# A hybrid attention block: six of the projection's nine column chunks in seven-product blocks, and attention moved behind them

## The chip, the cores and the metric

One Trainium2 chip, one of its cores. The time is that of one execution on the device, in microseconds. Both kernels compute in float32: every matrix product is written as three products of a high and a low part (hi·hi, hi·lo, lo·hi).

## The reference

One layer over 512 tokens of width 2048 with two kinds of attention heads (A: 8 query heads on 2 key/value heads; B: 8 heads of their own):

```python
h = rmsnorm(x, g_mix)
qa, ka, va, qb, kb, vb = split(h @ w_in)        # 1024,256,256,1024,1024,1024 columns
out_a = rmsnorm(mixer_a(qa, ka, va, ...))       # q, k normed per head, axial rotary, softmax
out_b = rmsnorm(mixer_b(qb, kb, vb))            # partial rotary; three dilated windows, as one masked softmax
x = x + concat(out_a, out_b) @ w_out
h2 = rmsnorm(x, g_ffn); gate, up = split(h2 @ w_gate_up)
x = x + (silu(gate) * up) @ w_down
return rmsnorm(x, g_final)
```

## The kernel before

Tokens lie in NT = 4 tiles of 128 rows, x is held transposed in KD = 16 tiles. The program is a hand-ordered list of *units*. A unit multiplies one weight tile of 128 x 512. Units of the first two phases, the input projection (w_in, 9 chunks of 512 columns x 16 units) and the output projection (w_out, 4 chunks for A, then 4 for B, x 8 units), have 12 matmuls: 4 token tiles times 3 products (`mm3`). The feed-forward (w_gate_up, w_down) runs in column blocks (`ColBlock`): of two column halves and two row halves, seven products of sums and differences take the place of eight plain ones, so a unit has 6 matmuls and there are 7 x 8 units for each pair of 512-column chunks and 16 row tiles. Its weights are first added or subtracted on DVE (L771).

Every weight tile is split: ACT copies it to a rounded high part (`split_hi`, L235 or L734), DVE subtracts that to get the low part (`split_lo`, L240 or L737). `prepare` issues the splits some units ahead and the loads (SP's queue) further ahead.

Attention is cut into small *tasks* in one queue, `side`. After every unit the main loop runs **one** task. `push_head` writes the tasks of a head: `m0` (transpose q on PE and split it, `tq`; finish the head before last: `pv(3)`, `fin`), `tk` (the same for k), and four score tasks `ms(i)`. A score task holds, in this order, `score(i)` of the current head, `pt(i)` of the head before and `pv(i-1)` of the head before:

- `score(i)`: 3 matmuls on PE (tile sc), row maximum on DVE (nm), exponential with row sum on ACT, reciprocal on DVE (L447), and p scaled by it on DVE (L448)
- `pt(i)`: 4 transposes on PE (tile pt), high part pTh on ACT (L186), low part pTl on DVE (L187)
- `pv(i-1)`: 3 matmuls on PE (tile o) that read pTh and pTl of the task before.

q and k of A are normed and turned on DVE (`push_norm_rope`, L312 to L328, two tasks for each of four token tiles), q and k of B turned by `rope_partial` (L383 to L387). Every engine takes its instructions in the order in which they are written. All q, k, v stay in SBUF, or go straight from PSUM into split form (`post_kvA`, `post_vB`); tasks of a head are queued as soon as its chunk of the projection is done.

Of the kernel before, what the change touches and what calls it, by code (L numbers as in the profile page):

```python
# [19 lines left out]
P = 128  # L20
# [30 lines left out]
RAWS = {"raw": 6, "craw": 24, "craw40": 23, "draw6": 22, "draw8": 28}  # L51
# [4 lines left out]
EVICT = 6  # L56

# [6 lines left out]
def encoder_block(ctx, tc, x, g_mix, w_in, g_q_a, g_k_a, g_out_a, g_out_b, w_out, g_ffn,  # L64
# [6 lines left out]
    sm = ctx.enter_context(tc.tile_pool(name="small", bufs=1))  # L71
# [14 lines left out]
    def wslot(tag):  # L86
        if tag == "wa":
            ring[0] += 1
            return home(16 + ring[0] % 12)
        return sp.tile([P, 512], F32R, tag=tag, bufs=W_TILES[tag], name=nm("w"))  # L90
# [4 lines left out]
    def small(base, n=4):  # L95
        return sm.tile([P, 16], F32, tag="t", bufs=24, name=nm(base))[:, :n]
# [7 lines left out]
    ident = cp.tile([P, P], F32, name="ident")  # L104
    gm = cp.tile([P, KD], F32, name="gm")
    gf = cp.tile([P, KD], F32, name="gf")
    go = cp.tile([P, KD], F32, name="go")
    mask = cp.tile([P, S + S - P], F32, name="mask")
    ropeb = cp.tile([P, 2, NT, PARTIAL], F32, name="ropeb")
    ones = cp.tile([P, 1], F32, name="ones")  # L110
    mhalf = cp.tile([P, 16], F32, name="mhalf")
    gqk = cp.tile([P, 2, HD], F32, name="gqk")
# [5 lines left out]
    def home(n):  # L118
        return form_tile(n % 7, n // 7).rearrange("p a b -> p (a b)")
# [5 lines left out]
    warm = slot("warm", BF16, (P, 512))  # L125
# [26 lines left out]
    def load_consts():  # L152
        for i, g in enumerate((g_q_a, g_k_a)):
            nc.sync.dma_start(gqk[:, i, :], row_bcast(g, HD))
        yield
# [3 lines left out]
        yield  # L159
        nc.sync.dma_start(ropeb, c_partial)  # L160
        yield
        nc.sync.dma_start(mask, c_mask)
        yield
# [9 lines left out]
    def rsqrt_mean(ss, n, count, name):  # L173
        t = small(name + "m", n)
        nc.vector.tensor_scalar(t, ss, 1.0 / count, EPS, op0=OP.mult, op1=OP.add)
        r = small(name, n)
# [3 lines left out]
    def split(src, name, gain=None, between=None, at=None):  # L180
        if at is None:
            hi, lo = slot(name + "h", F32R), slot(name + "l", F32R)
        else:
            hi, lo = home(at), home(at + 1)
# [3 lines left out]
        else:  # L188
            nc.scalar.activation(hi, src, AF.Copy, scale=gain)
            if between is not None:  # L190
                between()
# [62 lines left out]
    xT = [None] * KD  # L254
    ssx = slot("ssx")

    def x_transposes(k):
        ps = bank("xt")
        for t in range(NT):
            nc.tensor.transpose(ps[:, t * P:(t + 1) * P], xs[k][:, t, :], ident)  # L260
        if k == 0:
            xT[k] = split(ps, "xT", gm[:, k:k + 1], at=0)
            nc.scalar.activation(ssx, ps, AF.Square)
        else:
            sq = slot("xsq")
            xT[k] = split(ps, "xT", gm[:, k:k + 1], lambda: nc.scalar.activation(sq, ps, AF.Square), 2 * k)
            nc.gpsimd.tensor_tensor(ssx, ssx, sq, op=OP.add)
# [9 lines left out]
    def make_r1():  # L277
        r1["r"] = rsqrt_mean(col_sums(ssx), NT, D, "r1")
        r1["rs"] = small("r1s")
# [4 lines left out]
    def push_tables():  # L284
        for i, name in enumerate(("k", "q")):
# [15 lines left out]
            side.extend(lambda a=a, f=part: f(a) for a in range(3))  # L301

    def push_norm_rope(q0, dst, t, nh, name):
# [3 lines left out]
        def first():  # L307
            gs = tabs[name][1]
            tmp = st["tmp"] = slot("ra")
            ss = small("ssq")  # L310
# [4 lines left out]
            st["rs"] = rsqrt_mean(ss[:, :nh], nh, HD, "rq")  # L315
# [7 lines left out]
        def second():  # L323
            gc = tabs[name][0]
# [5 lines left out]
        side.extend((first, second))  # L330

    qA, kA, kTA, vA = {}, [], {}, {}
    vB, qkB = {}, {}
    kTA_done = []

    def post_kvA(ps):
        for j in range(2):
            vA[j] = tuple(home(48 + 2 * j + i).rearrange("p (a b) -> p a b", a=2) for i in range(2))
        for t in range(NT):
            r = r1["r"][:, t:t + 1]  # L340
            k0 = slot("kA")
            src = ps[t][:, 256:]
            h, l = vA[t // 2]
            nc.scalar.activation(h[:, t % 2, :], src, AF.Copy, scale=r)
            nc.scalar.activation(k0[:, :256], ps[t][:, :256], AF.Copy, scale=r)
            nc.vector.scalar_tensor_tensor(l[:, t % 2, :], src, r, f32(h[:, t % 2, :]), op0=OP.mult, op1=OP.subtract)
            kA.append(k0)
        for t in range(NT):
            push_norm_rope(kA[t][:, :256], kA[t][:, 256:], t, NKV, "k")
        wait(1)  # L350
        for kv in range(NKV):
            side.append(lambda kv=kv: transpose_k_a(kv))

    def transpose_k_a(kv):
# [3 lines left out]
        kTA[kv] = split(ps, "kT", at=52 + 2 * kv)  # L358

    def post_qA(j, ps):  # L360
        for t in range(NT):
            q0 = slot("qA")
            nc.scalar.activation(q0, ps[t], AF.Copy, scale=r1["r"][:, t:t + 1])
            push_norm_rope(q0, q0, t, 4, "q")
            qA[j, t] = q0
        wait(2)
        for h in range(4):
            push_head(("A", 4 * j + h))

    def post_vB(j, ps):  # L370
        for t in range(NT):
            r = r1["r"][:, t:t + 1]
            h, l = home(32 + 2 * (NT * j + t)), home(33 + 2 * (NT * j + t))
            nc.scalar.activation(h, ps[t], AF.Copy, scale=r)
            nc.vector.scalar_tensor_tensor(l, ps[t], r, f32(h), op0=OP.mult, op1=OP.subtract)
            vB[j, t] = (h, l)

    def rope_partial(q0, t):
        rot = q0.rearrange("p (h d) -> p h d", h=4)[:, :, :PARTIAL]
        tmp = sm.tile([P, 4, PARTIAL], F32, tag="rope", bufs=2, name=nm("rope"))  # L380
# [7 lines left out]

    def post_qkB(j, ps):
        for t in range(NT):  # L390
            q0 = qkB[j, t] = slot("qkB")
            nc.scalar.activation(q0[:, :256], ps[t][:, :256], AF.Copy, scale=r1["rs"][:, t:t + 1])
            nc.scalar.activation(q0[:, 256:], ps[t][:, 256:], AF.Copy, scale=r1["r"][:, t:t + 1])
        for t in (0, 2):
            side.append(lambda t=t: (rope_partial(qkB[j, t], t), rope_partial(qkB[j, t + 1], t + 1)))
        wait(1)
        for h in range(2):
            push_head(("B", 2 * j + h))
# [7 lines left out]
    class Head:  # L406
# [5 lines left out]
        def tq(self):  # L412
            ps = bank("qt")
            for t in range(NT):
                if self.kind == "A":
                    src = qA[self.h // 4, t][:, (self.h % 4) * HD:(self.h % 4 + 1) * HD]
                else:
                    src = qkB[self.h // 2, t][:, (self.h % 2) * HD:(self.h % 2 + 1) * HD]
# [3 lines left out]
        def tk(self):  # L422
# [4 lines left out]
            for t in range(NT):  # L427
                lo = 256 + (self.h % 2) * HD
                nc.tensor.transpose(ps[:, t * P:(t + 1) * P], qkB[self.h // 2, t][:, lo:lo + HD], ident)
            self.k = split(ps, "kT")  # L430

        def score(self, t):
            if t == 0:
                self.negm, self.z, self.rz = small("nm"), small("z"), small("rz")
# [13 lines left out]
            nc.vector.tensor_scalar(p, p, rz, None, op0=OP.mult)  # L448
# [10 lines left out]
        def pv(self, kb):  # L459
# [5 lines left out]
            else:  # L465
                v = cols(vB[self.h // 4, kb], (self.h % 4) * HD)
            mm3(self.o, v, self.pTs.pop(kb), kb == 0, kb == NT - 1)

        def fin(self):
# [12 lines left out]
            if self.h == 7:  # L482
                wait(1)
                side.append(lambda: row_rms(self.kind))
# [3 lines left out]
    def row_rms(kind):  # L488
        ro[kind] = rsqrt_mean(col_sums(acc[kind]), NT, NHA * HD, "ro")

    def push_head(spec):
        n = len(heads)
        heads.append(Head(*spec))

        def at(i, f, *a):
            return (i, f, a)
# [4 lines left out]
        def m0():  # L501
            cur.tq()
            if prev2:
# [9 lines left out]
        side.append(m0)  # L513
        side.append(cur.tk)
        for i in range(NT):
            side.append(lambda i=i: ms(i))
        if n == 15:
# [8 lines left out]
            side.append(t0)  # L526
            for i in range(NT):
                side.append(lambda i=i: tail(i))
# [4 lines left out]
            side.append(t5)  # L533
# [15 lines left out]
    def in_chunk(pieces, post):  # L549
        box = {}  # L550

        def mm(u, k):
            if k == 0:
                box["ps"] = [bank("pj") for _ in range(NT)]
            for t in range(NT):
                mm3(box["ps"][t], cols(xT[k], t * P), u.w, k == 0, k == KD - 1)
        add_chunk(w_in, [k * P for k in range(KD)], pieces, mm, lambda: post(box["ps"]), tag="wi")

    QB, KB, VB = 1536, 2560, 3584
    in_chunk([(1024, 0, 512)], post_kvA)  # L560
    in_chunk([(0, 0, 512)], lambda ps: post_qA(0, ps))
    in_chunk([(512, 0, 512)], lambda ps: post_qA(1, ps))

    def qk_pieces(j):
        return [(QB + 256 * j, 0, 256), (KB + 256 * j, 256, 256)]
    in_chunk([(VB, 0, 512)], lambda ps: post_vB(0, ps))
    in_chunk(qk_pieces(0), lambda ps: post_qkB(0, ps))
    in_chunk(qk_pieces(1), lambda ps: post_qkB(1, ps))
    in_chunk([(VB + 512, 0, 512)], lambda ps: post_vB(1, ps))
    in_chunk(qk_pieces(2), lambda ps: post_qkB(2, ps))  # L570
    in_chunk(qk_pieces(3), lambda ps: post_qkB(3, ps))

    x1 = {}
    oS = {}
    ss2 = small("ss2", 16)

    def drain_until(cond):
        while not cond():
            side.popleft()()

# [3 lines left out]
    def out_chunk(kind, c):  # L584
# [4 lines left out]
        def early(k):  # L589
            if (kind, k) not in oS:  # L590
                drain_until(lambda: (kind, k) in oT)
                oS[kind, k] = split(oT.pop((kind, k)), "oS", go[:, base + k:base + k + 1],
                                    at=42 + 2 * k if k < 7 else 35)

        class Back:
# [8 lines left out]
            def split(self):  # L604
                oS[kind, self.k] = split(self.t, "oS", go[:, base + self.k:base + self.k + 1],
                                         at=2 * self.k + (0 if kind == "A" else 42))
# [47 lines left out]
    def pair_sums(w):  # L654
# [3 lines left out]

        def tt(out, x, y, op=OP.subtract):
# [469 lines left out]
```

## Time and profile before

| what | value |
|---|---|
| time, median of 3 runs | 2025.89 us (2025.15 to 2027.72) |
| the profiled execution | 2026.94 us, its span 2025.2 us |
| mean granted TensorE clock | 0.997 |
| PE busy | 2005.7 us (99%), 9123 instructions |
| DVE busy | 1474.1 us (73%) |
| ACT busy | 1051.6 us (52%) |
| POOL busy | 134.9 us (7%) |

The input projection with most of the attention behind it ends near 590 us, the output projection near 720 us, and the feed-forward takes the rest. PE is the matrix engine, DVE and ACT are the two elementwise engines. A duration of a row in the timeline overlaps that of the next row on the same engine: what an instruction costs its engine is the distance from its start to the next start.

### The profile page before, as it was taken

The page shows a single profiled execution, that of the slowest core. Times are in us where ns is not written, and L with a number is a line of the kernel's source. Part 1 is how long each engine was busy: PE and PEld are TensorE (multiplying, and loading weights), DVE is VectorE, ACT ScalarE, POOL GpSimd, SP SyncE. Part 2 cuts the span into 40 slices and gives each one's busy share as a digit, 9 for nine tenths or more (in the row PEclk, how much of TensorE's full clock was granted, in tenths as well). Part 3 has the DMA queues.
Part 4 walks back from the last instruction along what each step waited for, and adds up shares of the span by engine and source line. Part 5 has one row for each costly group of instructions (what it writes and reads, how often), then busy time and mean ns, then how long its engine had stood idle before and what let it go on. Part 6 is the DMA issues. An engine that isn't in the chain of part 4 may idle for free. (4 is left out here: it accounts for less than half of the span.)

```text
span 2025.2 us, 26727 instructions
## 1 busy us (share of the span) xinstructions
PE 2005.7 (99%) x9123; PEld 1652.5 (82%) x9123; DVE 1474.1 (73%) x2596; ACT 1051.6 (52%) x1872; POOL 134.9 (7%) x149
## 2 busy tenths in 40 slices
PE   9999999999999999999999999999999999999997
PEld 7888888888888888888888888888888887788885
DVE  5555755554754688878877878878779987887876
ACT  5324344443543565555555555555556665666655
POOL 3100100000000000000000000000000121111121
PEclk9999999999999999999999999999999999999998
DMA  7322322223433546657558567467477799768754
GB/s 236 106 80 70 98 74 73 79 78 96 147 113 130 205 142 217 206 167 267 193 195 267 166 222 255 152 221 253 153 253 254 207 248 265 205 158 256 212 124 165
DMA packets 210360, 354.90 MB, mean 175 GB/s; under 512 B 19072, under 2 KB 63920, under 8 KB 210224
## 3 DMA queue, kind: packets, MB, share of 16 engines
q1 hardware_dynamic: 189440, 304.10, 45.9%
q0 software_dynamic: 12544, 25.17, 7.0%
q10 hardware_dynamic: 8240, 23.93, 3.5%
q8 instruction: 71, 1.16, 0.2%
q14 instruction: 65, 0.53, 0.1%
HBM read 300.97 MB, written 52.17 MB: 174 GB/s over the span
## 5 line engine op out<-in xcount | busy, mean ns | idle before, releaser
L734 ACT ACTIVATE tw<-raw 128x512 fp32r<-128x512 f32 x924 | 559.3, 628 | 442.5 <-DVE raw L771 280.7
L737 DVE TENSOR_TENSOR tw<-raw,tw 128x512 fp32r<-128x512 f32 x924 | 619.1, 686 | 173.4 <-ACT tw L734 169.5
L197 PE MATMUL zc<-tw,arena 128*128 128x512 f32 x1056 | 416.1, 394 | 2.0 <-ACT ev L907 1.9
L198 PE MATMUL zc<-tw,arena 128*128 128x512 f32 x1056 | 413.6, 392 | 3.5 <-DVE tw L737 3.5
L199 PE MATMUL zc<-tw,arena 128*128 128x512 f32 x1056 | 413.1, 391 | 0.0
L771 DVE TENSOR_TENSOR raw<-raw,raw 128x512 f32<-128x512 f32 x528 | 361.3, 684 | 0.5 <-DMA raw<-in_w_gate_up_dram 0.5
L198 PEld LDWEIGHTS zc<-tw,arena 128*128 128x128 f32 x1056 | 199.3, 189 | 46.7 <-DVE tw L737 6.5
L197 PEld LDWEIGHTS zc<-tw,arena 128*128 128x128 f32 x1056 | 199.1, 189 | 43.9 <-ACT ev L907 3.0
L199 PEld LDWEIGHTS zc<-tw,arena 128*128 128x128 f32 x1056 | 199.1, 189 | 41.5
L197 PE MATMUL pj<-w,arena 128*128 128x512 f32 x576 | 229.0, 398 | 1.2 <-ACT w L235 1.2
L198 PE MATMUL pj<-w,arena 128*128 128x512 f32 x576 | 224.8, 390 | 0.9 <-DVE w L240 0.9
L199 PE MATMUL pj<-w,arena 128*128 128x512 f32 x576 | 225.5, 391 | 0.1
L198 PE MATMUL yc<-tw,arena 128*128 128x512 f32 x528 | 206.0, 390 | 0.8 <-DVE tw L737 0.8
L197 PE MATMUL yc<-tw,arena 128*128 128x512 f32 x528 | 206.8, 392 | 0.0
L199 PE MATMUL yc<-tw,arena 128*128 128x512 f32 x528 | 205.8, 390 | 0.0
L240 DVE TENSOR_TENSOR w<-raw,w 128x512 fp32r<-128x512 f32 x176 | 130.8, 753 | 21.4 <-ACT w L235 13.6
L908 POOL DMA_DIRECT2D x1d<-ev x76 | 67.4, 990 | 1155.3 <-ACT ev L907 1149.4
L235 ACT ACTIVATE w<-raw 128x512 fp32r<-128x512 f32 x176 | 106.5, 627 | 56.1 <-PE pj L199 32.0
L199 PEld LDWEIGHTS pj<-w,arena 128*128 128x128 f32 x576 | 108.2, 188 | 23.9 <-DVE arena L192 0.5
L197 PEld LDWEIGHTS pj<-w,arena 128*128 128x128 f32 x576 | 108.3, 188 | 23.6 <-ACT w L235 1.4
L198 PEld LDWEIGHTS pj<-w,arena 128*128 128x128 f32 x576 | 108.5, 188 | 23.2 <-DVE w L240 1.2
L198 PEld LDWEIGHTS yc<-tw,arena 128*128 128x128 f32 x528 | 99.2, 188 | 21.8 <-DVE tw L737 1.6
(189 smaller groups left out, 2539.0 us busy)
## 6 DMA issues: line engine op xcount, KB each, us to landing
raw<-in_w_gate_up_dram SPq DMA_DIRECT2D x616, 256.0 KB, 4.5
raw<-in_w_down_dram SPq DMA_DIRECT2D x176, 256.0 KB, 6.7
forms<-pair SPq DMA_DIRECT2D x22, 896.0 KB, 5.2
raw<-in_w_in_dram SPq DMA_DIRECT2D x38, 512.0 KB, 3.7
x1d<-ev POOLq DMA_DIRECT2D x76, 256.0 KB, 6.6
fr<-forms ACTq DMA_DIRECT2D x35, 512.0 KB, 4.5
raw<-in_w_in_dram SPq DMA_DIRECT2D x68, 256.0 KB, 3.0
raw<-in_w_out_dram SPq DMA_DIRECT2D x32, 512.0 KB, 4.9
```

The costliest lines, as they stand in the source:

```text
L197: nc.tensor.matmul(dst, ah, bh, start=start, stop=False, skip_group_check=chained)
L198: nc.tensor.matmul(dst, ah, bl, start=False, stop=False, skip_group_check=chained)
L199: nc.tensor.matmul(dst, al, bh, start=False, stop=stop, skip_group_check=chained)
L235: nc.scalar.activation(self.w[0], src, AF.Copy)
L240: nc.vector.tensor_tensor(self.w[1], self.src, f32(self.w[0]), op=OP.subtract)
L734: nc.scalar.activation(self.pair[:, 0], self.src, AF.Copy)
L737: nc.vector.tensor_tensor(self.pair[:, 1], self.src, f32(self.pair[:, 0]), op=OP.subtract)
L771: nc.vector.tensor_tensor(t[dst], t[src[0]], t[src[1]], op=OP.add if form == "m6" else OP.subtract)
L908: nc.gpsimd.dma_start(x1_dram[2 * cb + j, row], e, accum_op=OP.add)
```

## The change

- Three pairs of chunks of the input projection (qA0+qA1, vB0+vB1, qB0+kB0) run as `ColBlock`s with seven products (`in_block`); kvA stays plain in front of them, qB1 and kB1 stay plain behind them. For this, x also gets sums and differences of its tile pairs (`x_prep`, `x_sums`, `x_split`) during the first chunk; one of x's plain parts that these overwrite goes to DRAM and comes back before qB1.
- All results of the projection are scaled, stored to DRAM from POOL's queue (`store`) and loaded back for attention on SP's queue (`reload`, `load_vB`).
- Attention begins only after the three blocks: `attention_tasks` queues all 161 tasks there, and over the next 64 units (qB1, kB1, and the four A chunks of the output projection) the loop runs `HEAD_RATE` = 2.7 tasks a unit.
- In `score`, p is scaled by the reciprocal on ACT and no longer on DVE.
- The row sums of squares for the first norm come from x loaded again by rows (4 x 1 MB) and squared on ACT with a row sum; before, POOL added squares of the transposed x, and PE summed them.
- v of B is split on ACT and DVE from the reloaded copy, one more task a head.
- Small tiles share one SBUF tile; two rings of weight buffers are a little shorter (`craw40` 23 to 20, `draw6` 22 to 20).

```diff
+HEAD_RATE = (2.7, 2.7)
+COLUMN_BLOCKS = 3
...
-            nc.vector.tensor_scalar(p, p, rz, None, op0=OP.mult)
+            nc.scalar.activation(p, p, AF.Copy, scale=rz)
...
+    in_plain("kvA", 1024)
+    groups = [(("qA0", "qA1"), (0, 512)), (("vB0", "vB1"), (VB, VB + 512)), (("qB0", "kB0"), (QB, KB)),
+              (("qB1", "kB1"), (QB + 512, KB + 512))]
+    for names, lo in groups[:COLUMN_BLOCKS]:
+        in_block(names, lo)
+    last = blocks[-1]
+    last.after("m7", 1, lambda: nc.gpsimd.dma_start(arena[0][:, 1], ar_dram))
+    last.after("m5", 0, load_consts)
+    last.after("m3", 0, lambda: side.extend(attention_tasks()))
...
+    attend = [len(units)]
+    for names, lo in groups[COLUMN_BLOCKS:]:
+        for name, c in zip(names, lo):
+            in_plain(name, c)
...
-        if side:
+        credit = credit + HEAD_RATE[n >= attend[1]] if attend[0] <= n < attend[2] else 1.0
+        while side and credit >= 1.0:
             side.popleft()()
+            credit -= 1.0
```

The new task list of a head, and the order in which the lists follow:

```diff
+        tasks = [m0] + ([cur.tk] if cur.kind == "B" else [])
+        tasks.extend(lambda i=i: ms(i) for i in range(NT))
...
+        todo = [lambda: reload("kvA", kA), lambda: reload("qA0", qA[0])] + table_tasks()
+        for t in range(NT):
+            todo += [lambda t=t: split_vA(t)]
+            todo += norm_rope(lambda t=t: (kA[t][:, :256], kA[t][:, 256:]), t, NKV, "k")
+        k_turns = [lambda kv=kv: transpose_k_a(kv) for kv in range(NKV)]
+        todo += q_tasks(0) + k_turns
+        for h in range(4):
+            todo += head_tasks(("A", h))
+            if h == 1:
+                todo += [lambda: reload("qA1", qA[1])]
+            if h == 2:
+                todo += q_tasks(1)
...
+        for h in range(8):
+            if h < 7:
+                todo.append(lambda h=h: load_vB(h + 1))
+            todo.append(lambda h=h: split_vB(h))
+            todo += head_tasks(("B", h))
```

DVE, two score tasks of an A head in the program before; sc is the score tile, nm its negative row maximum, rz the reciprocal of the row sum, pTl the low part of the transposed p, w a weight's low part:

```order
L440 TENSOR_REDUCE nm_2345<-sc_2435 128x1
L447 RECIPROCAL rz_2347<-z_2346 128x1
L448 TENSOR_SCALAR p_2439<-p_2439,rz_2347 128x512
L187 TENSOR_TENSOR pTl_2450<-pt_2444,pTh_2449 128x512
L240 TENSOR_TENSOR w_2408<-raw_2238,w_2407 128x512
L440 TENSOR_REDUCE nm_2345<-sc_2476 128x1
L447 RECIPROCAL rz_2347<-z_2346 128x1
L448 TENSOR_SCALAR p_2480<-p_2480,rz_2347 128x512
```

DVE, three score tasks of an A head in the changed program (nm, z and rz are now parts of smalls):

```order
L490 TENSOR_REDUCE smalls<-sc_3896 128x1
L497 RECIPROCAL smalls<-smalls 128x1
L193 TENSOR_TENSOR pTl_3911<-pt_3905,pTh_3910 128x512
L490 TENSOR_REDUCE smalls<-sc_3918 128x1
L497 RECIPROCAL smalls<-smalls 128x1
L193 TENSOR_TENSOR pTl_3933<-pt_3927,pTh_3932 128x512
L490 TENSOR_REDUCE smalls<-sc_3939 128x1
L497 RECIPROCAL smalls<-smalls 128x1
L193 TENSOR_TENSOR pTl_3954<-pt_3948,pTh_3953 128x512
L244 TENSOR_TENSOR w_3881<-raw_3482,w_3880 128x512
```

A weight split stands now behind two or three score tasks and no longer behind each, and the scaling of p has left DVE. ACT at the same two places, the program before (pTh is the high part of the transposed p):

```order
L441 ACTIVATE p_2439,z_2346<-sc_2435,nm_2345 128x512
L186 ACTIVATE pTh_2449<-pt_2444 128x512
L235 ACTIVATE w_2456<-raw_2238 128x512
L441 ACTIVATE p_2480,z_2346<-sc_2476,nm_2345 128x512
L186 ACTIVATE pTh_2490<-pt_2485 128x512
```

and the changed one:

```order
L491 ACTIVATE p_3900,smalls<-sc_3896,smalls 128x512
L498 ACTIVATE p_3900<-p_3900,smalls 128x512
L192 ACTIVATE pTh_3910<-pt_3905 128x512
L491 ACTIVATE p_3922,smalls<-sc_3918,smalls 128x512
L498 ACTIVATE p_3922<-p_3922,smalls 128x512
L192 ACTIVATE pTh_3932<-pt_3927 128x512
```

The scaling (L498) stands between the exponential and pTh, which before followed one another. PE at that place in the changed program; o is the product of p and v:

```order
L203 MATMUL sc_3896<-arena_75,qTl_3848 128x512
L504 MATMUL pt_3905<-fixed,p_3714 128x128
L504 MATMUL pt_3905<-fixed,p_3732 128x128
L504 MATMUL pt_3905<-fixed,p_3754 128x128
L504 MATMUL pt_3905<-fixed,p_3793 128x128
L201 MATMUL o_3914<-pTh_3874,arena_75 128x512
L202 MATMUL o_3914<-pTl_3875,arena_75 128x512
L203 MATMUL o_3914<-pTh_3874,arena_75 128x512
L201 MATMUL sc_3918<-arena_75,qTh_3847 128x512
```

Before, the twelve matmuls of a unit stood between the last two of these groups; now the next score follows at once.

More of the change, by code (lines that the diff above doesn't have):

```diff
@@ L183, in split @@
         else:
-            hi, lo = home(at), home(at + 1)
+            hi, lo = (place(*h) for h in at)
         if gain is None:
@@ L260, in x_transposes @@
             nc.tensor.transpose(ps[:, t * P:(t + 1) * P], xs[k][:, t, :], ident)
+        i, half = divmod(k, 2)
+        if half == 0:
+            xpair[i] = sp.tile([P, 4 * 512], F32, tag="xpair", bufs=3, name=nm("xpair"))
+        flat = xpair[i][:, half * 1024:half * 1024 + 512]
+        view = flat.rearrange("p (f c) -> p f c", c=256)
+        hi, lo = (arena[half][:, 0:2, i, j] for j in range(2))
+        gain = gm[:, k:k + 1]
         if k == 0:
-            xT[k] = split(ps, "xT", gm[:, k:k + 1], at=0)
@@ L502, in m0 @@
             cur.tq()
+            if cur.kind == "A":
+                cur.tk()
             if prev2:
```

519 lines of the change are left out of this document (294 added, 225 removed).

## The prediction

> **What bounds the kernel now.** I read the page's busy times first, then the engines by stretches (the window view), then the timeline of single stretches.
>
> ```profile
> PE 2005.7 (99%) x9123; PEld 1652.5 (82%) x9123; DVE 1474.1 (73%) x2596; ACT 1051.6 (52%) x1872; POOL 134.9 (7%) x149
> ```
>
> The windows, each row: stretch, length, then busy time and count of PE, PEld, DVE, ACT, POOL, the granted clock, DMA:
>
> ```profile
> 0.00:52.00 52.00, 48.12 (x228) 37.08 (x229) 29.29 (x41) 26.59 (x49) 16.98 (x17) 1.00 0.77 238
> 52.00:340.00 288.00, 288.00 (x1344) 238.02 (x1343) 164.43 (x377) 113.92 (x233) 21.57 (x20) 1.00 0.28 83
> 340.00:590.00 250.00, 250.00 (x1203) 206.49 (x1202) 143.16 (x334) 111.66 (x230) 11.69 (x9) 1.00 0.32 99
> 720.00:1120.00 400.00, 400.00 (x1803) 331.30 (x1803) 331.26 (x549) 216.61 (x370) 1.33 (x1) 1.00 0.62 206
> ```
>
> PE never rests from 52 us on, in the attention (second and third row: DVE at 57%) as in the seven-product blocks (last row: DVE at 83%, and PE is still fed). So a matmul taken out is worth its full issue distance, and any wait that the change brings to PE counts in full. The issue distances, from PE's timeline in the attention of B:
>
> ```profile
> 479.85 0.39 PE L197 MATMUL pj<-w,arena 128*128 128x512 f32 x1
> ...
> 482.35 0.39 PE L199 MATMUL pj<-w,arena 128*128 128x512 f32 x1
> ...
> 486.48 0.60 PE L454 MATMUL pt<-ident,p 128*128 128x128 f32 x4
> 486.83 0.48 PE L197 MATMUL pj<-w,arena 128*128 128x512 f32 x1
> 487.15 0.39 PE L198 MATMUL pj<-w,arena 128*128 128x512 f32 x1
> ...
> 494.24 0.39 PE L197 MATMUL sc<-kTh,qTh 128*128 128x512 f32 x1
> ```
>
> Eleven steps between the first two rows take 2.50 us: 0.227 us a matmul, 2.7 us a unit. Four transposes take 0.35 us and lengthen the matmul behind them by 0.09: 0.44.
>
> **The chain inside a score task.** DVE and ACT in one score task of before:
>
> ```profile
> 495.12 0.69 DVE L444 CUSTOM_DVE_ANT_0 p<-sc,mask 128x512 f32<-128x512 f32 x1 [1.10 <-PE sc L199]
> ...
> 496.71 0.16 DVE L447 RECIPROCAL rz<-z 128x1 f32<-128x1 f32 x1 [0.89 <-ACT p L446]
> 496.90 0.49 DVE L448 TENSOR_SCALAR p<-p,rz 128x512 f32<-128x512 f32 x1
> 497.31 0.69 DVE L187 TENSOR_TENSOR pTl<-pt,pTh 128x512 fp32r<-128x512 f32 x1
> 497.91 0.69 DVE L240 TENSOR_TENSOR w<-raw,w 128x512 fp32r<-128x512 f32 x1
> ```
>
> ```profile
> 495.86 0.72 ACT L446 ACTIVATE p<-p,nm 128x512 f32<-128x512 f32 x1 [2.75 <-DVE nm L444]
> ...
> 496.58 0.58 ACT L186 ACTIVATE pTh<-pt 128x512 fp32r<-128x512 f32 x1
> 497.06 0.62 ACT L235 ACTIVATE w<-raw 128x512 fp32r<-128x512 f32 x1
> ```
>
> DVE's maximum at 495.12, ACT's exponential at 495.86, DVE's reciprocal at 496.71 (DVE idles 0.89 for it, though pTl and a weight split stand behind: it takes them in order), scaling at 496.90, pTl at 497.31, free at 497.91. One task thus holds DVE for 2.79 us, waits included. PE spends 1.8 us on a task (six matmuls, four transposes) and 2.7 on the unit that follows each: 4.5. The chain is hidden, with 1.1 us left after the weight split.
>
> In the changed program the scaling is ACT's, between the exponential and pTh. The DVE loop of one task then runs through both engines one after the other: maximum to exponential 0.74, to reciprocal 0.85, on to the scaling 0.19, scaling, pTh, pTl, and only behind pTl the next maximum. For the scaling on ACT the nearest row is
>
> ```profile
> L974 ACT ACTIVATE x<-x,rf 128x512 f32<-128x512 f32 x11 | 7.1, 712 | 3.0 <-POOL rf L177 2.0 <-POOL rf L993 1.0
> ```
>
> 0.71, less the 0.10 by which ACT rows overlap (pTh lasts 0.58, the next starts after 0.48): 0.61. It could be as short as DVE's 0.41 or the full 0.71. From a high part's start on ACT to its low part's on DVE:
>
> ```profile
> 252.90 0.60 ACT L186 ACTIVATE qTh<-qt 128x512 fp32r<-128x512 f32 x1 [10.68 <-PE qt L419]
> ...
> 253.53 0.69 DVE L187 TENSOR_TENSOR qTl<-qt,qTh 128x512 fp32r<-128x512 f32 x1 [7.20 <-ACT qTh L186]
> ```
>
> 0.63, and pTl holds DVE 0.60. Sum 0.74+0.85+0.19+0.61+0.63+0.60 = **3.62 us** a task. And units no longer follow each task: two or three tasks run in a row, where PE has only 1.8 us of work for 3.62.
>
> **The sum, part by part.** (1) Three pairs of chunks need 7 x 8 x 6 = 336 matmuls in place of 384: 144 fewer, 144 x 0.227 = **-32.7 us**. The blocks are of the feed-forward's kind, which the row 720 to 1120 shows PE-bound; their DVE work (56 low parts, 32 sums, 6 closing updates a block) is at most what those have. Cost taken: none.
>
> (2) The attention stretch, 161 tasks. The order of DVE from the tables to the last pTl has 60 score tasks with a pt, 4 without, 4 last pTl, 34 splits of q, k, v, 58 weight splits, 8 q and 4 k norms, 16 partial rotations, 20 row updates and output splits. Their distances:
>
> ```profile
> 91.56 2.49 DVE L240 TENSOR_TENSOR w<-raw,w 128x512 fp32r<-128x512 f32 x4
> ...
> 105.37 0.29 DVE L312 CUSTOM_DVE_ANT_0 ra<-qA 128x128 f32<-128x128 f32 x1 [6.32 <-ACT qA L363]
> ...
> 110.42 0.28 DVE L312 CUSTOM_DVE_ANT_0 ra<-qA 128x128 f32<-128x128 f32 x1
> ...
> 63.90 0.28 DVE L312 CUSTOM_DVE_ANT_0 ra<-kA 128x128 f32<-128x128 f32 x1
> ...
> 67.46 0.28 DVE L312 CUSTOM_DVE_ANT_0 ra<-kA 128x128 f32<-128x128 f32 x1
> ...
> 468.54 0.35 DVE L383 TENSOR_TENSOR rope<-qkB,ropeb 128x64 f32<-128x64 f32 x2
> ...
> 469.46 0.35 DVE L383 TENSOR_TENSOR rope<-qkB,ropeb 128x64 f32<-128x64 f32 x2
> ...
> 649.92 2.72 DVE L624 SCALAR_TENSOR_TENSOR x<-pw,ro,x 128x512 f32<-128x512 f32 x4 [5.67 <-PE pw L199]
> ```
>
> Four splits in 2.49 with the last one's 0.69: 0.60 each. One q norm 5.05 less two splits: 3.85. One k norm 3.56 less two: 2.36. A rotation 0.92. Four row updates 2.72: 0.66 each. DVE in all: 60 x 3.62 = 217, 4 x 1.78 = 7, (4+34+58) x 0.60 = 58, 8 x 3.85 = 31, 4 x 2.36 = 9, 16 x 0.92 = 15, 20 x 0.66 = 13: **350 us**. PE over the same rows of its order: 1086 matmuls and 90 groups of transposes, 247 + 40 = **286 us**. All 350 are DVE's own order and its waits for ACT; none is filled by a later instruction. So PE waits at least 64 us, less what DVE may lead by when the stretch begins (its splits stand some three units ahead: 8 us): 56.
>
> On top come DVE's waits for PE at the change of a head. The first score needs qTl, and its maximum starts 0.88 us after it (494.24 to 495.12): 16 x 0.88 = 14. In nine of sixteen heads a unit stands between the q transposes and that score; two of these are covered by DVE's norms or rotations, the other seven cost 2.7 less the split, 2.1 each: 15. In B the k transposes and their high part come before that score, some 0.6 us in eight heads: 5. Waits in all 56 + 34 = **+90 us**.
>
> (3) The clock. After a thin stretch at the end of before it fell:
>
> ```profile
> 2000.00:2005.00 5.00, 3.29 (x12) 1.65 (x10) 5.00 (x9) 1.56 (x5) 0.00 (x0) 1.00 0.00 0
> 2005.00:2010.00 5.00, 3.97 (x10) 2.90 (x11) 3.36 (x9) 4.13 (x8) 1.44 (x2) 0.61 0.31 113
> 2010.00:2015.00 5.00, 5.00 (x17) 3.91 (x17) 1.28 (x5) 2.56 (x5) 0.54 (x1) 0.70 1.04 378
> ```
>
> Twelve matmuls in 5 us, 54% by their distance, and in the next 10 us 0.39 x 5 + 0.30 x 5 = 3.45 us of clock were lost. Between units the attention will have 1.8 of 3.62 us, 50%: much the same. If each head trips it once, 16 x 3.45 = 55 us; if the units refill PE in time, nothing. I take a quarter, **+14**, and keep both ends.
>
> The Trainium skill ("TensorE: Matmul & The Clock Gate", section "Why this matters for your kernels") says that the clock drops after gaps of over some 3 us without matmuls. The trace differs: it fell after a stretch with twelve matmuls in it. By that page only the start of the attention and the second group of q norms would trip it, two times 3.45, which makes 7 in place of 14.
>
> (4) The first chunk. A unit there takes PE 2.7 + 0.44 = 3.2 us, and the row 0 to 52 shows DVE and ACT at 29 and 27 of 52 us. The x sums are of the size of
>
> ```profile
> L660 DVE TENSOR_TENSOR pair<-pair 128x256 f32<-128x256 f32 x120 | 45.5, 421 | 26.8 <-ACT pair L682 25.8
> L734 ACT ACTIVATE tw<-raw 128x512 fp32r<-128x512 f32 x924 | 559.3, 628 | 442.5 <-DVE raw L771 280.7 <-PE zc L199 81.1 <-PE yc L199 40.9
> L884 ACT ACTIVATE arena<-fr 128x1024 fp32r<-128x1024 f32 x35 | 36.8, 1051 | 3.3 <-DMA fr<-forms 3.3
> ```
>
> so DVE gets 2 x 0.42 + 0.60 = 1.4 us more a unit and ACT 0.6: it fits. Four squares of 2048 elements on ACT don't: 0.63 and 0.42 more for each further 512, 1.9 us each, 8 in all, of which I take **+3** (0 to 8).
>
> (5) Stores, reloads, shorter rings. A store costs POOL about as much as
>
> ```profile
> L908 POOL DMA_DIRECT2D x1d<-ev x76 | 67.4, 990 | 1155.3 <-ACT ev L907 1149.4 <-DMA raw<-in_w_down_dram 5.4 <-ACT tw L734 0.3
> ```
>
> 1 us; 45 of them lie on an engine at 7%. The reloads are queued five tasks or more ahead of their use, and a late one would join a wait that is DVE's already. 161 tasks fit into 64 x 2.7 = 173, so none is left to run in a heap. Cost taken: none.
>
> Sum against the profiled execution: 2026.94 - 32.7 + 90 + 14 + 3 = 2101; that execution lies 1 above the median of the runs: **2100 us**, 3.7% slower.
>
> **Rivals.** *PE keeps the pace* (faster): the waits of DVE and ACT overlap as before, and only the norms stand bare: 17 us of q norms with three splits against three units (8), and some 3 us at the start: 2026.9 - 32.7 + 12 + 3 - 1 = **2008**. For it: DVE and ACT are far from busy in the stretch when waits aren't counted. Against it: DVE's order leaves nothing to run in the waits. It decides at the point where the waits equal the 33 us saved: a score task would have to hold DVE 2.7 us or less, not 3.62.
> *The clock falls in every head* (slower still): 2100 - 14 + 55 = **2141**. For it: the 54% row. Against it: a full unit after two or three tasks. The Trainium skill (the same page, "Part 4: PE-mode transpose") says that transposes do not count as PE activity for the clock, which speaks for this rival; no row here shows it.
> *Half of it*: the chain is right, but the waits at head changes hide behind it and the clock stays: 2026.9 - 32.7 + 56 + 3 - 1 = 2052, down to 2030 if the scaling takes only 0.41 (60 x 0.2 = 12) and DVE leads by more.
>
> **How the numbers follow.** Forecast 0.68 (2060 to 2125), clock in every head 0.14, half 0.10, PE keeps the pace 0.08. The range leaves out the faster rival and the lower end of the half: 2050 to 2142. About 0.2% is what a measurement of this kernel can tell from no change (its runs spread 0.13%). Faster 0.08, within 0.2% 0.02, slower 0.90.
>
> **What would show it.** In the profile after: PE at 100% in the three blocks, and about 64 us or more of PE idle between their end and the last pTl, released by DVE pTl and qTl; the distance from one maximum to the next on DVE near 3.6 where no unit stands between; ACT's scaling at 0.6 to 0.7. It is wrong if PE is full there, if the distance is below 2.7, or if the waits are named by DMA.

## The result and the profile after

| | before | after |
|---|---|---|
| median | 2026.31 us (2025.15 to 2027.72, 4 runs) | 2116.88 us (2115.26 to 2118.43, 4 runs) |
| ratio to before | 1 | 1.0447 (95% interval 1.0428 to 1.0465) |
| profiled execution, its span | 2026.94, 2025.2 | 2116.81, 2115.0 |
| matmul instructions on PE | 9123 | 8971 |

The change makes the kernel 4.5% slower: 91 us, where 74 had been forecast. The page's busy times after:

```profile
PE 2020.5 (96%) x8971; PEld 1636.9 (77%) x8971; DVE 1570.9 (74%) x2766; ACT 1166.0 (55%) x2024; POOL 139.1 (7%) x179
```

Where the time arises is read from a landmark that both kernels have, the first transposes of x1 in the output projection (the line of tile x1t, first of before, then of after; the two last times are the first and the last start):

```profile
L679 PE MATMUL x1t<-ident,x x64: 270/272/325, 654.4 to 734.1; 128*128 128x128 f32 x64
```

```profile
L897 PE MATMUL x1t<-fixed,x x64: 270/272/327, 745.5 to 825.1; 128*128 128x128 f32 x64
```

745.5 - 654.4 = 91 us: the whole loss lies ahead of it; behind it the changed kernel is 1 us shorter. The windows of after (columns as in the prediction) say where:

```profile
0.00:52.00 52.00, 50.15 (x232) 38.56 (x233) 31.24 (x61) 37.47 (x64) 4.13 (x11) 1.00 0.87 279
52.00:290.00 238.00, 234.12 (x1025) 191.20 (x1025) 188.35 (x315) 128.75 (x213) 16.34 (x29) 1.00 0.72 249
290.00:700.00 410.00, 337.18 (x1454) 254.45 (x1453) 223.09 (x561) 205.42 (x398) 35.08 (x36) 0.93 0.28 90
760.00:1160.00 400.00, 400.00 (x1819) 331.00 (x1818) 323.29 (x536) 219.91 (x378) 1.39 (x1) 1.00 0.58 199
```

The blocks (second row) are all but full, the feed-forward (last row) too. In the attention stretch PE stands idle for 410 - 337.18 = 73 us, and the granted clock loses 0.07 x 410 = 29. The two overlap: 58 us ran at half speed, and in 12 of these PE stood idle anyway (the rows from 390.50 in the last section show 7 of them), so that 23 of the 29 us count. The borders, in the timeline of before (the start of its second chunk)

```profile
61.85 0.50 PE L197 MATMUL pj<-w,arena 128*128 128x512 f32 x1
```

and of after (the first matmul of the three blocks, the first one behind them, the last low part of p; a bracket at the end of a row is the time for which the engine idled before it, and who ended that):

```profile
63.15 0.39 PE L201 MATMUL zc<-tw,arena 128*128 128x512 f32 x1
...
294.45 0.39 PE L201 MATMUL pj<-w,arena 128*128 128x512 f32 x1
...
704.88 0.69 DVE L193 TENSOR_TENSOR pTl<-pt,pTh 128x512 fp32r<-128x512 f32 x1 [0.44 <-ACT pTh L192]
```

The first chunk costs 63.15 - 61.85 = 1.3 us more. The blocks take 231.3 us, to 294.45, for what cost 1152 x 0.227 = 261.5 before: -30. That leaves +120 for the attention stretch. Counted directly it lasts to 705.6, 411 us for PE work that the prediction put at 286, so 125; the two counts agree to 5 us.

Who keeps PE waiting there (the largest waits, by the instruction that ended them: total, times, longest, us):

```profile
PE o L201 <- ACT pTh L192: 35.5, 29, 3.8
PE sc L203 <- DVE qTl L193: 16.7, 3, 8.9
PE sc L201 <- ACT kTh L192: 6.6, 5, 1.7
PE o L202 <- DVE pTl L193: 6.4, 28, 0.3
PE sc L201 <- ACT qTh L192: 3.1, 3, 1.6
```

All are ended by ACT and DVE, none by a DMA. And the chain itself, three score tasks in a row on DVE with no unit between them, and one round of it on ACT and PE:

```profile
440.14 0.69 DVE L490 TENSOR_REDUCE smalls<-sc 128x1 f32<-128x512 f32 x1 [4.66 <-PE sc L203]
441.67 0.16 DVE L497 RECIPROCAL smalls<-smalls 128x1 f32<-128x1 f32 x1 [0.84 <-ACT p L491]
443.11 0.69 DVE L193 TENSOR_TENSOR pTl<-pt,pTh 128x512 fp32r<-128x512 f32 x1 [1.27 <-ACT pTh L192]
443.71 0.68 DVE L490 TENSOR_REDUCE smalls<-sc 128x1 f32<-128x512 f32 x1
...
447.29 0.68 DVE L490 TENSOR_REDUCE smalls<-sc 128x1 f32<-128x512 f32 x1
```

```profile
441.07 0.60 PE L504 MATMUL pt<-fixed,p 128*128 128x128 f32 x4
...
441.87 0.72 ACT L498 ACTIVATE p<-p,smalls 128x512 f32<-128x512 f32 x1 [0.23 <-DVE smalls L497]
442.50 0.58 ACT L192 ACTIVATE pTh<-pt 128x512 fp32r<-128x512 f32 x1
...
443.13 0.49 PE L201 MATMUL o<-pTh,arena 128*128 128x512 f32 x1 [1.46 <-ACT pTh L192]
```

Maximum to maximum 3.57 and 3.58 us. Of that DVE works 1.4 and idles 2.1: 0.84 for the exponential, 1.27 for the scaling and the high part. The transposes of this round begin at 441.07, and ACT comes to them at 442.50, behind the scaling of another tile that nobody needs yet.

### The profile page after: what moved, and what is told of

Read it like the earlier page. It is cut to its first block, busy times and chain, and to the rows that moved or that the text cites. A ratio compares the mean times of both kernels' runs of the same rounds, so it can differ in the third digit from the quotient of the medians.

```text
span 2115.0 us, 27535 instructions
## 1 busy us (share of the span) xinstructions
PE 2020.5 (96%) x8971; PEld 1636.9 (77%) x8971; DVE 1570.9 (74%) x2766; ACT 1166.0 (55%) x2024; POOL 139.1 (7%) x179
## 5 line engine op out<-in xcount | busy, mean ns | idle before, releaser
L688 ACT ACTIVATE tw<-raw 128x512 fp32r<-128x512 f32 x1092 | 661.4, 628 | 531.4 <-DVE raw L725 343.5
L691 DVE TENSOR_TENSOR tw<-raw,tw 128x512 fp32r<-128x512 f32 x1092 | 731.0, 687 | 201.2 <-ACT tw L688 196.9
L201 PE MATMUL zc<-tw,arena 128*128 128x512 f32 x1248 | 490.2, 393 | 2.2 <-ACT ev L1038 1.7
L202 PE MATMUL zc<-tw,arena 128*128 128x512 f32 x1248 | 487.6, 391 | 4.5 <-DVE tw L691 4.3
L203 PE MATMUL zc<-tw,arena 128*128 128x512 f32 x1248 | 486.8, 390 | 0.0
L725 DVE TENSOR_TENSOR raw<-raw,raw 128x512 f32<-128x512 f32 x624 | 427.5, 685 | 1.7 <-DMA raw<-in_w_gate_up_dram 1.7
L202 PEld LDWEIGHTS zc<-tw,arena 128*128 128x128 f32 x1248 | 234.9, 188 | 56.3 <-DVE tw L691 9.0
L201 PEld LDWEIGHTS zc<-tw,arena 128*128 128x128 f32 x1248 | 234.7, 188 | 52.1 <-ACT ev L1038 2.4
L203 PEld LDWEIGHTS zc<-tw,arena 128*128 128x128 f32 x1248 | 234.7, 188 | 49.0
L201 PE MATMUL yc<-tw,arena 128*128 128x512 f32 x624 | 243.9, 391 | 0.0
L202 PE MATMUL yc<-tw,arena 128*128 128x512 f32 x624 | 243.1, 390 | 0.8 <-DVE tw L691 0.8
L203 PE MATMUL yc<-tw,arena 128*128 128x512 f32 x624 | 242.9, 389 | 0.0
L202 PEld LDWEIGHTS yc<-tw,arena 128*128 128x128 f32 x624 | 117.2, 188 | 25.5 <-DVE tw L691 1.6
L203 PEld LDWEIGHTS yc<-tw,arena 128*128 128x128 f32 x624 | 117.1, 188 | 24.4
L201 PEld LDWEIGHTS yc<-tw,arena 128*128 128x128 f32 x624 | 117.2, 188 | 24.0
L201 PE MATMUL xc<-tw,arena 128*128 128x512 f32 x312 | 121.7, 390 | 0.0
L202 PE MATMUL xc<-tw,arena 128*128 128x512 f32 x312 | 121.5, 389 | 0.1
L203 PE MATMUL xc<-tw,arena 128*128 128x512 f32 x312 | 121.4, 389 | 0.0
L193 DVE TENSOR_TENSOR pTl<-pt,pTh 128x512 fp32r<-128x512 f32 x64 | 44.2, 692 | 82.4 <-ACT pTh L192 82.4
L201 PE MATMUL pj<-w,arena 128*128 128x512 f32 x192 | 80.4, 419 | 2.5 <-ACT arena L283 2.5
L202 PE MATMUL pj<-w,arena 128*128 128x512 f32 x192 | 78.2, 407 | 0.3 <-DVE w L244 0.3
```

The source lines that it names most:

```text
L193: nc.vector.tensor_tensor(lo, src, f32(hi), op=OP.subtract)
L201: nc.tensor.matmul(dst, ah, bh, start=start, stop=False, skip_group_check=chained)
L202: nc.tensor.matmul(dst, ah, bl, start=False, stop=False, skip_group_check=chained)
L203: nc.tensor.matmul(dst, al, bh, start=False, stop=stop, skip_group_check=chained)
L688: nc.scalar.activation(self.pair[:, 0], self.src, AF.Copy)
L691: nc.vector.tensor_tensor(self.pair[:, 1], self.src, f32(self.pair[:, 0]), op=OP.subtract)
```

## Experiments

Each was timed in three rounds next to the kernel before (medians of it 2025.8 to 2026.7 us).

**The scaling back on DVE**, in the changed kernel:

```diff
-            nc.scalar.activation(p, p, AF.Copy, scale=rz)
+            nc.vector.tensor_scalar(p, p, rz, None, op0=OP.mult)
```

> The changed kernel with one edit undone: p is scaled by DVE again, not by ACT. Theory (one chain through DVE and ACT holds each score task): the distance from one row maximum to the next on DVE, where no unit stands between, falls from 3.57 to 2.79 us, the 60 tasks save about 45 us, and the time is near 2070 us (2050 to 2085; the clock may add to it). Rival (the sum of DVE's work in the attention stretch sets the time): 64 scalings of 0.41 us come back to DVE, 26 us more work on it, and the time is near 2140 us.

Measured 2076.11 us, ratio 1.0243 (1.0228 to 1.0258). DVE in three tasks without a unit between:

```profile
446.28 0.69 DVE L490 TENSOR_REDUCE smalls<-sc 128x1 f32<-128x512 f32 x1 [0.45 <-PE sc L203]
...
449.02 0.68 DVE L490 TENSOR_REDUCE smalls<-sc 128x1 f32<-128x512 f32 x1
...
451.74 0.68 DVE L490 TENSOR_REDUCE smalls<-sc 128x1 f32<-128x512 f32 x1
```

2.74 and 2.72 us instead of 3.57. The window of the stretch:

```profile
290.00:700.00 410.00, 362.10 (x1651) 281.66 (x1650) 268.51 (x659) 176.98 (x366) 38.53 (x38) 0.97 0.33 106
```

The task is 0.85 shorter and the kernel 41 us, 64 x 0.64: PE idles 48 us in the window in place of 73, and the clock is 0.97 in place of 0.93, some 25 and 16 us. DVE's work went up, so it isn't the sum of DVE's work that sets the stretch. ACT's work went down by 64 scalings, but ACT was busy in only 205 of the 410 us, and the experiment after the next wins more with ACT's work unchanged. One line of the change is 45% of its net loss.

**The same line alone in the kernel before**, the other way round:

```diff
-            nc.vector.tensor_scalar(p, p, rz, None, op0=OP.mult)
+            nc.scalar.activation(p, p, AF.Copy, scale=rz)
```

> The kernel before, with p scaled by ACT instead of DVE and nothing else changed. Chain theory: in the kernel before a task has a whole unit beside it, 1.8 + 2.7 = 4.5 us of PE, and the chain with ACT's scaling is about 3.6 us, with a weight split 4.2: still hidden. Expected 2026 us, within 0.2% (2024 to 2031). Rival (the scaling on ACT costs its time in every task wherever it stands, as the 41 us between the changed kernel and its version with DVE's scaling suggest): 2026 + 41 = 2067 us.

Measured 2035.64 us, 1.0046 (1.0031 to 1.0061): neither, but far nearer to the first (4 us above its range). PE's waits in the attention there, its two largest:

```profile
PE o L197 <- ACT pTh L186: 2.3, 3, 0.9
PE o L198 <- DVE pTl L187: 1.7, 7, 0.3
```

With one unit beside each task the longer chain costs 9 us instead of 41. It isn't hidden altogether. The two rows show 4 us; the landmark x1t shows more, 665.9 in this run's profile against 654.4 before. Of these 11.5 us, 1.4 arise in the first chunk, where the clock was 0.97 over the first 52 us, and 5 are idle time of PE in the attention. The other 5 lie in rows that count as busy, at the same few waits (the section on the prediction says what a wait costs beyond its idle time). Behind the landmark the profile regains 1.5 us.

**The chain broken up.** The reciprocal and the scaling of score i-1 move into task i, the high part of p goes ahead of the scaling on ACT, and the low part behind the maximum on DVE (`rcp` is the reciprocal, `norm` the scaling, `pt_hi` the transposes with the high part, `pt_lo` the low part):

```diff
+            if i:
+                cur.rcp(i - 1)
+            if prev:
+                prev.pt_hi(i)
+            if i:
+                cur.norm(i - 1)
             cur.score(i)
             if prev:
-                prev.pt(i)
+                prev.pt_lo(i)
```

> The changed kernel with the same instructions in another order inside a score task: reciprocal and scaling of score i-1 stand in task i, the high part of the transposed p ahead of the scaling, its low part behind the row maximum, so that no engine waits for the other inside a task. (Two rings of weight buffers are one step shorter, and v is loaded two tasks later, to fit.) Theory (the chain): a task takes about 1.8 us on either engine, PE sets the pace there, and of some 125 us of waits about 35 are left (q norms, first scores of heads): 2025 us (2005 to 2050). Rival (the engines' work, or the clock alone): no instruction is gone, so the time stays within 20 us of 2117.

Measured 2068.74 us, 1.0202 (1.0181 to 1.0222): 48 us won with the same instructions, half of the 92 that I expected and outside my range. What is left, by the waits and the window:

```profile
PE pt L508 <- ACT p L503: 13.4, 5, 6.7
PE sc L201 <- ACT kTh L192: 10.2, 7, 2.4
```

```profile
290.00:700.00 410.00, 369.76 (x1677) 293.67 (x1676) 237.20 (x593) 219.84 (x438) 37.60 (x38) 0.95 0.32 101
```

A head's last reciprocal now stood in the next head's first task, behind q norms on DVE, and the k transposes of B are waited for. The clock still lost 0.05 x 410 = 20 us.

**More PE work in each task**: every score computed twice (192 matmuls more, 44 us of PE).

```diff
             mm3(ps, cols(self.q, t * P), self.k, True, True)
+            mm3(ps, cols(self.q, t * P), self.k, True, True)
```

> The changed kernel with each score's three matmuls done twice (the second three overwrite the first): 192 matmuls more, 44 us of PE work in the attention stretch, nothing on DVE or ACT. Theory (the chain holds the tasks and PE waits; part of the loss is the clock, which falls when PE is thinly used): most of the 44 us goes into the waits; with the clock at full speed for longer the time is 2105 to 2130 us. Rival (PE's own work sets the stretch): 2117 + 44 = 2161 us.

Measured 2135.96 us, 1.0542 (1.0526 to 1.0558): +19 of 44, and 6 us above my range. 25 of the 44 us cost nothing, since they ran where PE had waited (its waits for pTh fell from 35.5 to 19.6 us) and the clock in the window of 290 to 700 was 0.94 in place of 0.93. PE does not set the stretch alone, but it is not idle at every place where work is added.

**More units beside the attention**: two blocks and 1.7 tasks a unit (48 matmuls more, 11 us).

```diff
-HEAD_RATE = (2.7, 2.7)
-COLUMN_BLOCKS = 3
+HEAD_RATE = (1.7, 1.7)
+COLUMN_BLOCKS = 2
```

> Two chunk pairs in seven-product blocks in place of three, and 1.7 tasks a unit in place of 2.7, so that the 161 tasks spread over 96 units. PE gets 48 matmuls more, 11 us. (One ring of weight buffers is two tiles shorter, to fit.) Theory (waits come from tasks that run without a unit between): DVE's order and PE's work in the stretch are then alike (some 370 us each), waits fall from some 125 to about 45 us, and the time is near 2050 us (2030 to 2070). Rival (the stretch costs what its tasks cost, however they are spread): 2117 + 11 = 2128 us.

Measured 2091.09 us, 1.0322 (1.0304 to 1.0339): 26 us won, not 67, and outside my range. PE's waits for pTh are 23.7 us in place of 35.5: a unit between two tasks takes away what it covers. That the rest stands where two tasks still meet (1.7 a unit) is my reading; it was not traced place by place.

**The waits at the change of a head taken away, the chain left as it is.** The q and k transposes of the next head go into the third and second score task of this one, the norms and rotations stand singly between tasks:

```diff
+            if i in (1, 2) and n < 15:
+                (heads[n + 1].tk, heads[n + 1].tq)[i - 1]()
-        tasks = [m0] + ([cur.tk] if cur.kind == "B" else [])
+        tasks = [m0]
```

> The changed kernel, score tasks as they are; the q and k transposes of the next head are issued in the second and third score task of the head before, the norms of q's second group and the rotations of B stand one by one between score tasks instead of in a heap, and weight rings are a little shorter. Theory (PE's waits at the change of a head are a term of their own, next to the chain): the waits named by qTl, kTh, qTh (16.7 + 6.6 + 3.1 = 26 us) go, and some 10 of the 29 us of clock with them: 2117 - 36 = 2081 us (2070 to 2095). Rival (DVE's row of instructions and waits sets the length of the whole stretch, so the same time turns up as waits for the high and low parts of p): 2105 to 2117 us.

Measured 2117.04 us, 1.0443 (1.0426 to 1.0460): nothing. The rival was right, and the waits tell how:

```profile
PE o L201 <- ACT pTh L192: 51.4, 26, 5.2
PE pt L504 <- DVE pTl L193: 9.6, 8, 1.9
PE o L202 <- DVE pTl L193: 5.0, 22, 0.2
...
PE sc L203 <- DVE qTl L193: 1.3, 1, 1.3
```

```profile
290.00:700.00 410.00, 337.80 (x1437) 258.88 (x1436) 217.78 (x558) 203.14 (x397) 35.32 (x36) 0.90 0.27 87
```

The 26 us named by qTl, kTh and qTh are down to 2, and the waits for the high part of p went from 35.5 to 51.4: taken from one name, given to another. PE's idle time in the window is 72 us, as before. The clock got worse, 0.90 in place of 0.93, some 12 us; since the time stayed the same, about as much was won in rows that count as busy, which was not traced. There was a second possible cause: the 153 tasks that are left, at 2.7 a unit, end some seven units early, so that these units hide nothing. Two runs with the tasks spread over all 64 units, of this version (2.42 a unit) and of the changed kernel (2.53 a unit):

> The prefetch alone (2117 us, as the changed kernel), its 153 tasks spread over all 64 units at 2.42 a unit. With 2.7 they ended some seven units before the last, and these stood beside nothing. Theory (the score chain on DVE sets the length of the stretch, whatever stands beside it): 6.5 more units run inside the same length, 6.5 x 2.7 = 18 us less 6.5 x 0.6 = 4 for their splits on DVE: 2103 us (2098 to 2108). Rival 1 (the waits at the change of a head are a term of their own, and only the packing hid the gain): 2117 - 36 = 2081 us or less. Rival 2 (the rate does nothing): 2114 to 2119.

> The changed kernel with its 161 tasks spread over all 64 units, 2.53 a unit instead of 2.7, and weight rings as in the version before. Theory (the score chain sets the length): four more units inside the same stretch, 4 x (2.7 - 0.6) = 8 us less: 2109 us (2104 to 2112). Rival (PE's waits go with the number of tasks, not with the units beside them): 2115 to 2119 us.

Measured 2107.65 us, 1.0397 (1.0382 to 1.0413), and 2113.90 us, 1.0436 (1.0418 to 1.0453). Spreading the tasks is worth 9 and 3 us: the first lies inside the theory's range, the second 2 us outside it, between theory and rival. Prefetch and spread together win 6 us over the spread alone, where 36 had been named.

**Both cures together**: the chain broken up, the prefetch, and the last reciprocal and scaling of a head (`last`) ahead of norms and rotations.

```diff
         def m0():
             if prev:
-                prev.rcp(3)
-                prev.norm(3)
-            cur.tq()
+                prev.last()
```

> The pipelined version (2069 us) with the same prefetch and spread, and with the last reciprocal and scaling of a head ahead of any norm or rotation. Theory (its rest is what its waits name): waits for the scaled p (13.4), kTh (10.2) and qT (2.4) go, 26 us, and about 12 of its 21 us of clock: 2069 - 38 = 2031 us (2020 to 2045). Rival (PE's rest is spread thin over the tasks, and the clock falls whenever tasks follow each other without a unit, so little is won): 2055 to 2069 us.

Measured 2028.97 us, 1.0012 (1.0002 to 1.0021), as the theory had it. The same window and the largest waits:

```profile
290.00:700.00 410.00, 387.70 (x1845) 310.89 (x1844) 257.80 (x632) 240.72 (x471) 37.66 (x38) 0.99 0.36 116
```

```profile
PE o L202 <- DVE pTl L521: 9.7, 10, 2.6
PE pt L515 <- ACT p L510: 5.6, 3, 3.5
```

PE idles 22 us in place of 73, and the clock is 0.99. DVE works 258 us in place of 223 in the same 410: it waited less, and more units went by. The prefetch, which was worth nothing under the long chain, wins 40 us here (2068.74 to 2028.97) together with `last`. How these divide between the two was not run; the waits that they were aimed at were 10.2 us for kTh (prefetch) and 13.4 for the scaled p (`last`).

**The same with two blocks** (qA0+qA1 and qB1+kB1), and then both with their tasks spread over all units and `last` ahead of the split of v and of B's rotations too:

```diff
-HEAD_RATE = (2.7, 2.7)
+HEAD_RATE = (2.42, 2.42)
...
-HEAD_RATE = (1.7, 1.7)
+HEAD_RATE = (1.61, 1.61)
...
     def split_vB(h):
+        heads[7 + h].last()
```

> The pipelined, prefetching version with two column blocks instead of three (qA0+qA1 and qB1+kB1), so that 96 units instead of 64 stand beside the attention, 1.7 tasks a unit. Theory: 48 more matmuls than with three (11 us), but PE's waits nearly gone: 2026 - 33 + 11 + 15 = 2019 us (2010 to 2035). Rival (a rest of 40 us or more of waits and clock stays whatever the number of units, as with two blocks alone): 2045 us or more.

> The pipelined, prefetching version with three blocks (2029 us), its 153 tasks spread over all 64 units (2.42 a unit instead of 2.7, which left the last seven units without tasks), and a head's last reciprocal ahead of the split of v and of the rotations; the ring of raw weight tiles is 4 instead of 5. Theory (what it still loses is PE's 22 us of waits behind the blocks, most where three tasks follow each other): waits for the scaled p (5.6) go and a quarter of the rest, 2029 - 10 = 2019 us (2012 to 2025), faster than the kernel before. Rival (the waits are those of norms and rotations on DVE at the start and do not depend on the rate, or the shorter ring makes weights late): 2026 to 2035 us.

> The pipelined, prefetching version with two blocks (2030 us), its 153 tasks spread over all 96 units (1.61 a unit instead of 1.7), the same two edits beside it. It has 12 us of PE waits behind the blocks and 5 us of clock. Theory: 2030 - 6 = 2024 us (2019 to 2028). Rival (no change but the shorter ring): 2028 to 2035 us.

Measured: two blocks 2029.73 us, 1.0017 (1.0007 to 1.0026), inside the range and 11 us above what I expected; three blocks spread 2026.44 us, 1.0000 (0.9991 to 1.0009), which is the time of the kernel before again, 7 us short of what I expected and inside the rival's range; two blocks spread 2021.37 us, 0.9974 (0.9963 to 0.9985). By the medians the last one beats both kernels, by 5 us and by 95. In its window PE is idle 9 us:

```profile
290.00:700.00 410.00, 400.90 (x1922) 326.44 (x1921) 235.94 (x523) 241.87 (x468) 32.01 (x32) 0.99 0.37 118
```

Where the 5 us arise is open. The profiled executions (2023.44 us, and 2026.94 of the kernel before) do not show them in the part that was changed: x1t begins at 655.3 here, 0.9 later than in the kernel before.

```profile
L931 PE MATMUL x1t<-fixed,x x64: 270/272/330, 655.3 to 734.9; 128*128 128x128 f32 x64
```

These two profiles part only near the end of the feed-forward, where the clock of the kernel before fell (its row from 2005 in the prediction) and that of this version fell later, at 2014 us.

## Why the prediction was right, and where it was not

- *The saved matmuls (-32.7)*: right. The blocks took 231.3 us for 1008 matmuls, 228.8 at 0.227 us each; PE waited 1.3 for their weights.
- *The chain (3.62 a task)*: 3.57 measured. The versions in which it is shorter or broken up won 41 and 48 us of the 120, and 88 with the early transposes and `last` added, so its length is shown to be a cause of the loss, and the largest that was found. The prediction named DVE's pTl and qTl as what would end PE's waits. The rows name ACT's pTh first (35.5 us), which stands one step ahead of pTl in the same chain, and then qTl (16.7).
- *Waits (+90)*: 97, so the sum was nearly right. Of the 120 us, 23 are the clock's and 73 are PE's idle time. Some 18 more lie in rows that count as busy: what stands ahead of a wait isn't overlapped by the next row (0.39 us in place of 0.227 for a matmul, 0.60 in place of 0.35 for four transposes), at 82 waits; 6 I can't place. The parts of the sum were not right, and that it came out so near is in part luck: the change of a head was put at 34 us of its own, next to the chain's 56. Taking those waits away won 0 to 6 us. They lie beside the chain: what isn't waited for at a head's change is waited for in the next tasks, until the chain itself is broken up.
- *The clock (+14, bound 55)*: the term that was furthest off. The granted clock lost 29 us, half of the bound and not the quarter I took; 23 of them count. With 9 more for it, 7 more for the waits, 2.5 more for the blocks and 1.7 less for the first chunk, the forecast of 2100 becomes 2117, as measured. The 7 us that the prediction worked out from two long gaps are far too few: the clock fell eleven times.
- *The first chunk (+3)*: +1.3. *Stores and reloads (0)*: none of PE's waits in the stretch is named by a DMA.
- *PE keeps the pace* was to decide at 2.7 us a score task. With DVE's scaling the task takes 2.72 and the kernel still loses 50 us, so that point was set too high: the heads' changes and the clock have to go as well. With most of all three gone the kernel takes as long as the one before (2028.97 and 2026.44 us). *The clock falls in every head*: it fell eleven times in sixteen heads, and the result lies between the forecast and this rival. The rival leaned on the statement that transposes do not count as PE activity for the clock; the last section shows a step that speaks against it.

Not settled: why spreading the tasks won 2.5 us and not 10 in the last version with three blocks (PE's idle time in the window fell from 22 to 17 us, and the clock lost 1.7 us more), and where the 5 us of the last version with two blocks come from.

## What to carry to other kernels

When work is taken from the engine that is always busy, look up what that work was hiding: here 144 matmuls less were worth 30 us, and bringing the attention tasks closer together cost 120. Count the chain that one task makes through in-order engines, waits included, and compare it with the work of the other engine that stands beside it; if it is longer, a shorter chain (moving a step into the next task, and putting first on each engine what another one waits for) is worth more than a less busy engine. A list of waits by name says who came last, not what would be won by removing it: take two of them away together before you call one harmless.

## What the runs showed of the hardware

The clock falls though PE works. In the changed kernel's attention stretch it fell eleven times, for 3.4, 6.8 or 10.2 us, and every fall began on a fixed step of 3.41 us (332.47, 363.19, 390.50, 414.39 and so on). Windows on these steps, first at the longest wait (8.9 us, for norms of q), then a step that no fall followed, then around the three tasks shown above:

```profile
387.09:390.50 3.41, 1.22 (x6) 0.67 (x4) 3.20 (x15) 0.00 (x0) 1.11 (x1) 1.00 0.01 2
390.50:393.91 3.41, 0.00 (x0) 0.00 (x0) 3.34 (x14) 0.00 (x0) 1.10 (x2) 0.50 0.26 78
393.91:397.33 3.42, 0.09 (x1) 0.09 (x1) 3.28 (x5) 0.00 (x0) 1.33 (x2) 0.50 0.21 75
397.33:400.74 3.41, 3.41 (x12) 2.71 (x12) 1.31 (x3) 1.71 (x4) 0.00 (x0) 0.50 0.00 0
...
407.56:410.97 3.41, 2.33 (x12) 1.40 (x11) 1.42 (x3) 1.89 (x4) 0.00 (x0) 1.00 0.38 129
...
441.70:445.11 3.41, 1.75 (x6) 1.05 (x6) 1.42 (x3) 1.89 (x4) 0.00 (x0) 1.00 0.56 214
445.11:448.52 3.41, 3.09 (x9) 1.91 (x9) 1.45 (x3) 1.82 (x5) 0.00 (x0) 0.50 0.00 0
448.52:451.94 3.42, 3.42 (x10) 2.65 (x9) 1.45 (x3) 1.98 (x5) 0.00 (x0) 0.50 0.00 0
451.94:455.35 3.41, 3.41 (x18) 2.80 (x17) 0.78 (x2) 0.78 (x2) 0.00 (x0) 1.00 0.00 0
```

In the row from 441.70 PE was busy 1.75 of 3.41 us, with three products of o and three of sc and no gap of over 2 us; and the next 6.8 us ran at half speed. A unit in them took one matmul every 0.43 us in place of 0.227:

```profile
448.44 0.63 PE L201 MATMUL pj<-w,arena 128*128 128x512 f32 x1
448.87 0.63 PE L202 MATMUL pj<-w,arena 128*128 128x512 f32 x1
```

The Trainium skill ("TensorE: Matmul & The Clock Gate", "Why this matters for your kernels") names gaps of over some 3 us without matmuls; here, where the longest gap was under 2, it fell all the same.

What goes with the falls is PE's busy share in the step ahead. It was 0 to 54% ahead of all eleven; of the 93 other steps of the stretch at full clock only three lie below 55%. In the eleven other kernels with attention behind the blocks no fall followed a step of more than 54% either (82 falls). Transposes belong to that share: the step from 407.56 holds 21% of matmuls with 512 columns (at 0.227 us each), yet with its eight transposes PE was busy 68% of it, and no fall followed; the step from 441.70 holds 40% of such matmuls and was busy 51%. Why it is so no run here shows.

So a chain that leaves PE half idle is paid for twice: with 73 us of idle time went 29 us of granted clock, 23 of which count, and with 22 us of it 4.
